# A hybrid layer (short convolution and HGRN2): attention and norm steps put into other slots, and one low half of the weights subtracted on chip instead of stored

## The chip, the cores and the metric

The kernel runs on one core of a Trainium2 chip. The metric is the device time of one execution in microseconds (us). The engines are TensorE (PE, with PEld for its weight loads), VectorE (DVE), ScalarE (ACT), GpSimd (POOL) and SyncE (SP). POOL and SP also issue DMA transfers.

## The reference

One encoder layer over a prompt of 2048 tokens and a separate sample of 64 tokens, width 1024. Cut to what matters here (8 heads of 128, chunks of 64 tokens):

```python
h = rms_norm(x, g_pre)
vA, bA, cA, zA, q, f, iv, zB, gA, gB = split_cols(h @ w_in)
u = cA * vA
yA = (silu(zA) * bA * causal_conv3(u, conv_w)) @ w_a_out
fg = lb + (1 - lb) * sigmoid(f); logf = log(fg); k = 1 - fg
q = silu(q) * K_B ** -0.5; v = iv
# hgrn2, for each chunk of 64 tokens, b = cumsum(logf) within the chunk:
att = causal((q * exp(b - ref)) @ (k * exp(ref - b)).T)
o = att @ v + (q * exp(b)) @ S
S = exp(b_last) * S + (k * exp(b_last - b)).T @ v
o = o * rsqrt(mean(o * o) + EPS) * g_onorm
yB = (o * silu(zB)) @ w_b_out
x = x + rms_norm((sigmoid(gA) * yA + sigmoid(gB) * yB) @ w_o, g_post)
x = x + (p @ w_ple_proj) * sigmoid(rms_norm(x, g_ple) @ w_ple_gate)
# returned: x of both, the last two columns of u and the last state S of both
```

## The kernel before

All activations stand feature-major (features on partitions, tokens along the row). The 2112 tokens run in three blocks of 768, 704 and 640 (block 0, block 1, the last block), each through the whole layer. Every product is split: an operand is cast to fp32r (`hi`) on ACT and the rest (`lo = x - hi`) is subtracted on DVE (`split`, L230). A weight block then takes three matmuls for each slice of k: hi by hi (L454), hi by the activations' lo (L455) and lo by hi (L456).

The projections work on pairs of column groups with seven products instead of eight (Strassen and Winograd's scheme): A11, S3, S1, S2, A12, A22, S4, where A11, A12 belong to the first column group, A21, A22 to the second, and S1 to S4 are sums of them. One product is 4 slices of k by 3 matmuls, 12 matmuls. `sgroup` runs such a group, `combined` gets its weights. In block 0 (`first`) the four raw halves are loaded, the sums are made on DVE, and the sums and the low halves are stored to DRAM through SP (`low<-lo` and `S<-s` in the views). Later blocks load what was stored (`kept_w`, `split_w`: raw half, cast on ACT, low half by a DMA); `used_later` tells which low halves are stored, and `spread` makes one be subtracted again. Raw, hi, lo and sum tiles come from rings of few buffers (5, 4, 4 and 3).

Path B runs head by head (`path_b`). `head_prep` does the groups of one head, FF/IV (forget gate and values) and ZB/QQ (output gate and queries), and starts the turning of keys and values: DVE transposes 32x32 pieces (L1067), POOL stores them (`tk<-r`, `tv<-r`, L1069), reads them back by token (`r<-tk`, L1074) and copies the keys side by side (L1080). The attention of the head runs while the next head's groups run: scores, then PE makes the state updates from keys and values (L1144), DVE scales and adds the states chunk by chunk (`p_state`, L1156 and L1159), and PE makes the outputs from scores and states (L1182, L1184). The outputs are normed, transposed back (`turn_o`, `to<-r`), read (`read_o`, `r<-to`) and multiplied with the output gate (`scale_o`, L1221).

These steps are placed by slots: after each product PE's group calls `hook`, which runs one slot's steps. A head has 21 slots in block 0 (a third group, of the gates, runs there) and 14 in the later blocks; `at(slot, step)` fills them. In block 0 there are also `piece`s in the slots: steps of `prepare_sums`, which make weight sums for later. The slots fix the order of PE's matmuls; around them a scheduler puts each engine's instructions in order. Each engine runs its instructions in that order, so a wait holds up all that stands behind it.

Between two blocks the norm of the finished block (L709, L721 are its transposes on PE) runs in the slots of the next block's first gate groups; `spread_out` takes the number of its steps for each slot from a row of figures.

Of the kernel before, what the change touches and what calls it, by code (L numbers as in the profile page):

```python
# [20 lines left out]
KB = D // P  # L21
# [10 lines left out]
VA, BA, CA, ZA, QQ, FF, IV, ZB, GA, GB = range(10)  # L32
# [62 lines left out]
def hybrid_step(  # L95
# [142 lines left out]
    def load_raw(src):  # L238
        raw = wp.tile([P, 4, P], F32, tag="raw", name=nm("raw"), bufs=5)
        SP.dma_start(raw, src)  # L240
        return raw
# [13 lines left out]
    def used_later(idx, part):  # L255

        if GA * 8 <= idx < GB * 8 + KB - 2:
            return part in ("S1", "S2", "S3", "S4")  # L260
        if idx in (GB * 8 + KB - 1, IV * 8):
            return part != 0
        if idx < QQ * 8:
            return part != 1
        if W_B <= idx < W_O:
            return part == 1 and idx - W_B >= KH
        return True

    def split_w(raw, key=None, spread=False, among_sums=False):


        hi = wp.tile([P, 4, P], F32R, tag="hi", name=nm("hi"))
        if spread:
            lo = low_tile()
            split(raw, hi, lo)
            return hi, lo
        if key in lows:
            lo = wp.tile([P, 4, P], F32R, tag="lo", name=nm("lo")) if among_sums else low_tile()
            A.copy(hi, raw)  # L279
            SP.dma_start(lo.bitcast(F32), lows[key])  # L280
            return hi, lo
        lo = wp.tile([P, 4, P], F32R, tag="lo", name=nm("lo"))
        split(raw, hi, lo)
        if key is not None and used_later(*key):
            lows[key] = dram.tile([P, 4, P], F32, tag=f"lo{key}", name=nm("low"), bufs=1)
            stores[0].dma_start(lows[key], lo.bitcast(F32))
        return hi, lo
# [53 lines left out]

    def kept_w(i1, i2, name, anew=False, spread=False):

        keys = dict(A11=(i1, 0), A12=(i1, 1), A22=(i2, 1))
        if name in keys:
            return split_w(load_raw(w_blk[keys[name]]), None if anew else keys[name], spread or keys[name][0] < QQ * 8 and keys[name][1] == 1)
        return split_w(load_raw(sums[i1][name]), (i1, name))

    def combined(i1, i2, first, anew):
# [598 lines left out]
    def head_prep(bl, hc, hd, first, hs, before):  # L948
# [22 lines left out]
        if hs and hd == 0:  # L971
            plain_group(FF * 8, IV * 8, hs, sink_f)
        else:
            sgroup(FF * 8 + hd, IV * 8 + hd, hc, sink_f, first)
        lg, staged_k, eq, staged_v = rt(), rt(turn * P), rt(), rt(turn * P)
        b, qx = staged_k[:, :n], staged_v[:, :n]
        wrote = [turned("tv", vt, staged_v, turn)]
# [248 lines left out]
    def path_b(bl, hc, first, kept, fills, hs, lead_sums=None):  # L1226


        def keep_z(hd, z):
            kept["o", hd] = spill("o", hd)  # L1230
            G.dma_start(kept["o", hd], z)

        slots, base, d = {}, 0, None
        if not first and not bl["last"]:
            next(fills)
        for hd in range(NH):
            d = head_prep(bl, hc, hd, first, hs, d)
            if first and hd > 0:
                next(fills, None)
            assert not hooks  # L1240
            attn = [head_attn(i, gs, d, hd) for i, gs in enumerate(bl["parts"])]
            scores = head_scores(bl["parts"], d)
            keep = partial(keep_z, hd, d["z"])
            piece = lead_sums and partial(next, lead_sums, None)

            def at(slot, *steps):
                slots.setdefault(base + slot, []).extend(s if callable(s) else partial(next, s) for s in steps if s is not None)

            if first:
                late = int(hd == 0)  # L1250
                at(2 + 2 * late, scores)
                for g in attn:
                    for slot in (6, 9, 12):
                        at(slot + late + (g is attn[1]), g)
                at(4 + late, partial(copy_k, d))
                at(15 + late, partial(turn_o, d))
                at(19 + late, partial(read_o, d))
                at(26 + late, partial(scale_o, d), keep)
                for slot in (8, 14, 20) if hd else (17,):
                    at(slot, piece)  # L1260
                if hd == NH - 1:
                    for slot in range(22, 94, 6):
                        at(slot, piece)
            else:
                for slot, steps in enumerate(((), (scores,), (), (), attn, (), attn)):
                    at(slot + 2, *steps)
                at(11, partial(turn_o, d))
                at(14, partial(read_o, d))
                at(14 + 7, partial(scale_o, d), keep)
                if hd == NH - 1:  # L1270
                    for slot in range(24, 108, 4):
                        at(slot, piece)
            count = 14 + 7 * first if hd + 1 < NH else 1 + max(slots) - base
            for slot in range(base, base + count):
                steps = slots.pop(slot, None)
                hooks.append(partial(each, steps) if steps else None)
            base += count
# [250 lines left out]
    def spread_out(*plans):  # L1528


        def steps(todo):
            with behind_all(m for m in copies + adds if m is not None):
                for gen, n in todo:
                    run(gen, n)

        for counts in zip_longest(*(plan for _, plan in plans), fillvalue=0):
            todo = [(gen, n) for (gen, _), n in zip(plans, counts) if n]
            hooks.append(partial(steps, todo) if todo else None)
# [131 lines left out]
    for bi, bl in enumerate(blocks):  # L1670
# [78 lines left out]
        if nxt:  # L1749
            xo.extend(stages[-1]["mid"])  # L1750
            fills = sized(nxt, gates(nxt, hc, kepts[bi + 1], False))
            norm = sized(bl, final_norm(bl, segs, xo, acc, h2, kept))
            spread_out((norm, (1, 1, 1, 1, 1, 1, 1, 0, 0, 0, 0, 1) + (0, 1) * KB + (0, 0, 1, 0, 0, 1) + (0, 1) * (KB - 1) + (1,)))
            run(fills, LEAD)
            assert not hooks
            run(final_gate(bl, segs, xo, h2, kept))
        else:

            gate = [final_gate(bl, [s], xo, h2, kept, anew=s is segs[1], held={} if s is segs[1] else {0: 0, 1: 0, 2: 0, 3: 2, 4: 0, 5: 4}) for s in segs]
            spread_out((norms[0], (2, 2, 1, 0, 1, 1, 4, 4)), (norms[1], (0,) * 6 + (1, 1) + (1, 1, 1, 0, 0, 1, 0, 1, 4, 4)))  # L1760
            run(ple(bl, ph, kept, spare=range(KB)))
            run(gate[0], 2)
            with behind_all(copies[:1]):
                run(norms[1], KB)
            run(gate[0])
            assert not hooks
            run(gate[1])
# [49 lines left out]
```

## Time and profile before

| what | value |
|---|---|
| time, median of three runs (lowest, highest) | 2527.51 us (2526.64, 2535.70) |
| the profiled execution's own time | 2528.36 us |
| its span in the profile | 2526.7 us |
| time around the span | 1.66 us |
| granted TensorE clock, mean | 0.999 |
| busy: PE, DVE, ACT, POOL | 2505.7, 1854.5, 1490.5, 477.6 us |
| DMA traffic | 761.36 MB, mean 301 GB/s |

The profile is of one execution. Block 0's heads run from about 99 to 475 us of the span, block 1's from about 1086 to 1345, the last block's from about 1860 to 2100. In a group's row stand line, engine, operation, output and input tiles, the size, the count, then busy us and mean ns, then the engine's idle us just before the group and what ended it.

### The profile page before, as it was taken

How to read it: one execution, taken by the hardware profiler on the slowest of the kernel's cores; microseconds unless marked ns; L12 is line 12 of the kernel's file. 1: busy time of each engine (PE TensorE's matmuls, PEld its weight loads, DVE VectorE, ACT ScalarE, POOL GpSimd, SP SyncE). 2: the span in 40 equal slices, each digit the busy share in tenths (PEclk: the TensorE clock that was granted, in tenths of full speed). 3: DMA queues.
4: the chain of work that ended last, by engine and by line, in shares of the span. 5: the costliest groups of instructions: out<-in, count | busy, mean ns of one | idle time of the engine just before them, and what ended most of it. 6: DMA issues, size and time to landing. Idle time of an engine off the chain costs nothing.

```text
span 2526.7 us, 47339 instructions
## 1 busy us (share of the span) xinstructions
PE 2505.7 (99%) x16302; PEld 2483.5 (98%) x16302; DVE 1854.5 (73%) x3575; ACT 1490.5 (59%) x2902; POOL 477.6 (19%) x819
## 2 busy tenths in 40 slices
PE   9999999999999999999999999999999999999999
PEld 9999999999999999999999999999999999999998
DVE  7898898998868775477775657978357775446967
ACT  6676676554453764466655556576356665546675
POOL 2032223221022021122223211102212221001011
PEclk9999999999999999999999999999999999999999
DMA  8789999997797798889989988989999998889986
GB/s 334 257 314 327 340 322 317 344 339 269 228 351 243 244 338 296 269 304 317 321 295 321 341 292 308 328 266 350 313 300 321 319 317 265 267 254 322 331 270 201
DMA packets 357873, 761.36 MB, mean 301 GB/s; under 512 B 44470, under 2 KB 49904, under 8 KB 357632
## 3 DMA queue, kind: packets, MB, share of 16 engines
q1 hardware_dynamic: 305856, 553.85, 64.8%
q0 software_dynamic: 51776, 204.48, 22.7%
q8 instruction: 128, 2.10, 0.3%
q14 instruction: 113, 0.93, 0.1%
HBM read 548.68 MB, written 209.47 MB: 300 GB/s over the span
## 4 chain that ended last, share of the span: by engine, by line
PE 87%; DVE 5%; DMA 4%; issue 2%; ACT 1%; POOL 1%; SPq 0%; DVEq 0%; ACTq 0%; POOLq 0%
PE pg L454 18%; PE pg L456 18%; PE pg L455 18%; PE pg L606 5%; PE pg L605 5%; PE pg L607 5%; PE pg L645 3%; PE pg L644 3%; PE pg L643 3%; DMA r<-tk 1%; PE pa L1144 1%; PE pa L1184 1%; PE pa L1182 1%; DMA low<-lo 1%; PE pa L1112 1%
## 5 line engine op out<-in xcount | busy, mean ns | idle before, releaser
L454 PE MATMUL pg<-r,hi 128*128 128x320 f32 (+2 forms) x3304 | 1076.5, 326 | 0.2 <-DVE r L502 0.2
L455 PE MATMUL pg<-r,hi 128*128 128x320 f32 (+2 forms) x3304 | 1067.4, 323 | 0.0
L456 PE MATMUL pg<-r,lo 128*128 128x384 f32 (+2 forms) x2380 | 777.1, 327 | 2.3 <-DMA lo<-low 1.2
L279 ACT CAST hi<-raw 128x512 fp32r<-128x512 f32 x658 | 405.0, 619 | 449.6 <-PE pg L455 186.3
L454 PEld LDWEIGHTS pg<-r,hi 128*128 128x128 f32 x3304 | 621.2, 188 | 2.5 <-issue 0.5
L455 PEld LDWEIGHTS pg<-r,hi 128*128 128x128 f32 x3304 | 621.7, 188 | 0.0
L456 PEld LDWEIGHTS pg<-r,lo 128*128 128x128 f32 x2380 | 447.2, 188 | 5.8 <-DVE lo L230 3.9
L230 ACT CAST hi<-raw 128x512 fp32r<-128x512 f32 x316 | 195.9, 623 | 179.6 <-PE pg L455 48.0
L456 PE MATMUL pg<-r,s 128*128 128x352 f32 (+1 forms) x924 | 291.7, 316 | 0.0
L606 PE MATMUL pg<-r,hi 128*128 128x320 f32 (+2 forms) x864 | 277.4, 322 | 0.3 <-DVE r L230 0.3
L605 PE MATMUL pg<-r,hi 128*128 128x320 f32 (+2 forms) x864 | 275.0, 322 | 0.0
L230 DVE TENSOR_TENSOR r<-r,r 128x320 fp32r<-128x320 f32 (+7 forms) x350 | 206.2, 608 | 42.9 <-ACT r L230 41.8
L230 DVE TENSOR_TENSOR lo<-raw,hi 128x512 fp32r<-128x512 f32 x263 | 180.2, 688 | 73.0 <-ACT hi L230 69.2
L230 ACT CAST r<-r 128x320 fp32r<-128x320 f32 (+7 forms) x350 | 183.8, 556 | 39.5 <-DVE r L1353 9.0
L607 PE MATMUL pg<-r,lo 128*128 128x352 f32 (+2 forms) x564 | 180.9, 321 | 0.4 <-DMA lo<-low 0.4
L456 PEld LDWEIGHTS pg<-r,s 128*128 128x128 f32 x924 | 173.5, 188 | 0.2 <-DVE s L230 0.2
L230 ACT CAST hi<-s 128x512 fp32r<-128x512 f32 x164 | 102.3, 624 | 120.7 <-PE pg L455 92.0
L644 PE MATMUL pg<-r,hi 128*128 128x384 f32 (+2 forms) x512 | 166.9, 327 | 0.2 <-DVE r L230 0.2
L643 PE MATMUL pg<-r,hi 128*128 128x384 f32 (+2 forms) x512 | 166.0, 328 | 0.2 <-ACT hi L279 0.2
L606 PEld LDWEIGHTS pg<-r,hi 128*128 128x128 f32 x864 | 162.1, 188 | 2.0 <-DVE r L230 1.5
L605 PEld LDWEIGHTS pg<-r,hi 128*128 128x128 f32 x864 | 161.3, 188 | 1.3 <-ACT r L230 0.8
L230 DVE TENSOR_TENSOR lo<-s,hi 128x512 fp32r<-128x512 f32 x164 | 112.4, 686 | 65.9 <-ACT hi L230 41.5
(383 smaller groups left out, 4174.5 us busy)
## 6 DMA issues: line engine op xcount, KB each, us to landing
raw<-w_blk SPq DMA_DIRECT2D x579, 256.0 KB, 4.6
raw<-S SPq DMA_DIRECT2D x436, 256.0 KB, 4.4
lo<-low SPq DMA_DIRECT2D x388, 256.0 KB, 4.4
s<-low SPq DMA_DIRECT2D x270, 256.0 KB, 4.8
low<-lo SPq DMA_DIRECT2D x239, 256.0 KB, 4.3
S<-s SPq DMA_DIRECT2D x152, 256.0 KB, 4.0
low<-r POOLq DMA_DIRECT2D x50, 256.0 KB, 5.0
r<-w_blk POOLq DMA_DIRECT2D x48, 256.0 KB, 7.1
```

What stands on the lines that cost most here:

```text
L230: return A.copy(hi, src).ins, V.tensor_tensor(lo, src, hi.bitcast(F32), ALU.subtract).ins
L279: A.copy(hi, raw)
L454: add(hi[:, k, :], xhi, start=start and k == 0, stop=False)
L455: add(hi[:, k, :], xlo, start=False, stop=False)
L456: last[0] = add(lo[:, k, :], xhi, start=False, stop=k == KH - 1).ins
L605: add(hi[:, k, :], xhi, start=start and k == 0, stop=False)
L606: add(hi[:, k, :], xlo, start=False, stop=False)
L607: last[0] = add(lo[:, k, :], xhi, start=False, stop=k == KH - 1).ins
L643: T.matmul(ps, hi[:, k % 4, :], xhi[:, c], start=k == ks[0], stop=False)
L644: T.matmul(ps, hi[:, k % 4, :], xlo[:, c], start=False, stop=False)
L645: last[0] = T.matmul(ps, lo[:, k % 4, :], xhi[:, c], start=False, stop=k == ks[-1]).ins
L1112: T.matmul(*unit, start=True, stop=True)
```

## The change

Four things. The low half of A22 of the groups FF/IV and ZB/QQ isn't stored in block 0 (`used_later`), and later blocks subtract it from the raw half on DVE (`among`); before, this was so only for the groups of lower number, path A's. The attention's steps from the states on come two slots later in block 0 and in the last block. In block 0 the pieces of `prepare_sums` move from slots 8, 14, 20 to 4, 10, 16. And one of the norm's early steps comes a slot later, with those behind it.

```diff
     def used_later(idx, part):
+        if idx // 8 in (QQ, IV) and part == 1:
+            return False
...
     def kept_w(i1, i2, name, anew=False, spread=False):
+        def among(idx, part):
+            return part == 1 and (idx < QQ * 8 or idx // 8 in (QQ, IV))
...
-            return split_w(load_raw(w_blk[keys[name]]), None if anew else keys[name], spread or keys[name][0] < QQ * 8 and keys[name][1] == 1)
+            return split_w(load_raw(w_blk[keys[name]]), None if anew else keys[name], spread or among(*keys[name]))
...
     # head_prep
-            sgroup(FF * 8 + hd, IV * 8 + hd, hc, sink_f, first)
+            sgroup(FF * 8 + hd, IV * 8 + hd, hc, sink_f, first, anew=hd == 0 and not bl["last"])
...
     # path_b, block 0 (first)
-                    for slot in (6, 9, 12):
+                    for slot in (6, 11, 14):
                         at(slot + late + (g is attn[1]), g)
                 at(4 + late, partial(copy_k, d))
-                at(15 + late, partial(turn_o, d))
-                at(19 + late, partial(read_o, d))
-                at(26 + late, partial(scale_o, d), keep)
-                for slot in (8, 14, 20) if hd else (17,):
+                at(17 + late, partial(turn_o, d))
+                at(21 + late, partial(read_o, d))
+                at(28 + late, partial(scale_o, d), keep)
+                for slot in (4, 10, 16) if hd else (17,):
                     at(slot, piece)
...
     # path_b, later blocks
-                for slot, steps in enumerate(((), (scores,), (), (), attn, (), attn)):
-                    at(slot + 2, *steps)
-                at(11, partial(turn_o, d))
-                at(14, partial(read_o, d))
-                at(14 + 7, partial(scale_o, d), keep)
+                late = 2 * bl["last"]
+                at(3, scores)
+                at(6 + late, *attn)
+                at(8 + late, *attn)
+                at(11 + late, partial(turn_o, d))
+                at(14 + late, partial(read_o, d))
+                at(21 + late, partial(scale_o, d), keep)
...
     # between blocks
-            spread_out((norm, (1, 1, 1, 1, 1, 1, 1, 0, 0, 0, 0, 1) + (0, 1) * KB + (0, 0, 1, 0, 0, 1) + (0, 1) * (KB - 1) + (1,)))
+            spread_out((norm, (1, 1, 1, 1, 1, 1, 0, 1, 0, 0, 0, 0, 1, 1) + (0, 1) * (KB - 1) + (0, 0, 1, 0, 0, 1) + (0, 1) * (KB - 1) + (1,)))
```

In instructions: SP issues 2078 where it issued 2126 (16 stores `low<-lo` and 32 loads of low halves fewer, 256 KB each), DVE runs 32 subtracts more, and the counts of PE, ACT and POOL are equal. On PE the matmuls L1182 and L1184 of every head of block 0 stand 24 matmuls later; in the last block so do L1144, L1182 and L1184; the norm's transposes L709 stand 12 rows later at both turns between blocks. Lines of the changed kernel have numbers five higher there than before.

The first place is DVE in the fourth head of block 0, where the states of the head before are scaled and added (L1159 before, L1164 now; `s_` and `lo_` are sums and low halves of weights). Before:

```order
L360 TENSOR_TENSOR s_3617<-raw_3605,raw_3607 128x512
L1221 TENSOR_TENSOR r_2040<-r_2852,r_2040 128x768
L230 TENSOR_TENSOR lo_3402<-s_3397,hi_3401 128x512
L495 TENSOR_TENSOR hf_3335<-hf_3217,pg_3234 128x384
L360 TENSOR_TENSOR s_3627<-raw_3607,raw_3609 128x512
L1156 COPY r_3343<-pa_3338 128x128
L1067 STREAM_TRANSPOSE r_3351<-r_3137 128x6x4x32
L1159 SCALAR_TENSOR_TENSOR r_3343<-r_3343,qc_2697,pa_3338 128x128 x3
L981 SCALAR_TENSOR_TENSOR r_3349<-keep,r_3348 128x768
L1159 SCALAR_TENSOR_TENSOR r_3447<-r_3343,qc_2697,pa_3444 128x128
```

And now:

```order
L230 TENSOR_TENSOR lo_3389<-s_3384,hi_3388 128x512
L500 TENSOR_TENSOR hf_3322<-hf_3198,pg_3216 128x384
L365 TENSOR_TENSOR s_3609<-raw_3589,raw_3591 128x512
L1161 COPY r_3330<-pa_3325 128x128
L1072 STREAM_TRANSPOSE r_3338<-r_3120 128x6x4x32
L1164 SCALAR_TENSOR_TENSOR r_3330<-r_3330,qc_2688,pa_3325 128x128
L1226 TENSOR_TENSOR r_2040<-r_2872,r_2040 128x768
L1164 SCALAR_TENSOR_TENSOR r_3330<-r_3330,qc_2688,pa_3325 128x128
L986 SCALAR_TENSOR_TENSOR r_3336<-keep,r_3335 128x768
L1164 SCALAR_TENSOR_TENSOR r_3330<-r_3330,qc_2688,pa_3325 128x128
```

The scale step of the head before (L1221, now L1226) stood ahead of the copy out of PSUM and the scan (L981, now L986) behind the third state; both now stand between the states.

The second place is DVE in the third head of block 1, from the reduced sums on to the transpose of the keys (L1067, now L1072), which opens their way to the state update. Before:

```order
L1012 TENSOR_TENSOR r_13947<-r_13737,r_13934 128x3x64
L1016 COPY r_13947<-hf_13946 128x128
L1018 TENSOR_TENSOR qc_13945<-qc_13945 128x5
L1067 STREAM_TRANSPOSE r_13935<-r_13947 128x6x4x32
L502 TENSOR_TENSOR r_13948<-hf_14005,hf_14024 128x352
```

And now, a row in the middle of the head and those at the transpose:

```order
L986 SCALAR_TENSOR_TENSOR r_13903<-keep,r_13902 128x704
L230 TENSOR_TENSOR s_13951<-raw_13948,hi_13950 128x512
L1173 TENSOR_SCALAR state_13899<-one_13892,r_13487 128x128
...
L1021 COPY r_13915<-hf_13914 128x128
L1023 TENSOR_TENSOR qc_13913<-qc_13913 128x5
L507 TENSOR_TENSOR r_13916<-hf_13973,hf_13992 128x352
L1072 STREAM_TRANSPOSE r_13903<-r_13915 128x6x4x32
```

The subtract of A22's low half (L230, into an `s` tile) is new between the scan and the states, and one step of the queries (L502, now L507) has come ahead of the keys' transpose.

The third place is POOL in a head of the last block (`to`, `tk`, `tv` are the turned outputs, keys and values in DRAM). Before:

```order
L1069 DMA to_24572<-r_24005 128x640
L1069 DMA tk_24540<-r_24399 128x640
L1074 DMA r_24498<-to_24572 128x4x160
L1074 DMA r_24610<-tv_24403 128x4x160
L1074 DMA r_24613<-tk_24540 128x4x160
L1080 COPY r_24615<-r_24613 128x640
```

And now:

```order
L1074 DMA tk_24480<-r_24350 128x640
L706 TENSOR_TENSOR ms_24510<-ms_24510,mhalf 128x4
L706 TENSOR_TENSOR ms_24519<-ms_24519,mhalf 128x1
L1079 DMA r_24578<-tv_24354 128x4x160
L1079 DMA r_24581<-tk_24480 128x4x160
L1074 DMA to_24571<-r_23956 128x640
L1085 COPY r_24583<-r_24581 128x640
L1079 DMA r_24509<-to_24571 128x4x160
```

The keys are now sent before the outputs, and the outputs are read back only behind the copy of the keys.

## The prediction

> **What bounds the kernel now.** I read the page first: the busy line, then the chain that ended last.
>
> ```profile
> span 2526.7 us, 47339 instructions
> PE 2505.7 (99%) x16302; PEld 2483.5 (98%) x16302; DVE 1854.5 (73%) x3575; ACT 1490.5 (59%) x2902; POOL 477.6 (19%) x819
> PE 87%; DVE 5%; DMA 4%; issue 2%; ACT 1%; POOL 1%; SPq 0%; DVEq 0%; ACTq 0%; POOLq 0%
> ```
>
> TensorE is busy 2505.7 of 2526.7 us, so it is the bound, and all its stops together are 21.0 us. The change alters no matmul (the instruction counts of PE are equal in the order of both kernels). So it can win back at most those 21 us and the little that PE loses around a stop; it can lose without such a limit. Next I read the groups of PE for what ends its stops. In a row the first pair of numbers is busy us and mean ns, the last part the idle us ahead of the group and its releaser.
>
> ```profile
> L456 PE MATMUL pg<-r,lo 128*128 128x384 f32 (+2 forms) x2380 | 777.1, 327 | 2.3 <-DMA lo<-low 1.2 <-DVE lo L230 1.0
> L1184 PE MATMUL pa<-r,r 128*128 128x128 f32 x208 | 41.2, 280 | 2.5 <-DVE r L1159 2.5
> L1144 PE MATMUL pa<-r,r 128*128 128x128 f32 x272 | 36.0, 276 | 4.3 <-POOL r L1080 4.2
> ```
>
> Three groups that the change can reach hold 9.1 of the 21 us: the attention's output waits for the states on DVE (L1184), the state update waits for POOL's copy of the keys (L1144), and projection products wait for the low half of a weight tile (L456). Windows tell where they lie.
>
> ```profile
> 99.00:475.00 376.00, 372.10 (x2410) 364.85 (x2409) 335.91 (x627) 248.74 (x521) 94.93 (x140) 1.00 0.90 322
> 452.00:700.00 248.00, 248.00 (x1459) 247.84 (x1456) 218.46 (x380) 130.10 (x266) 44.47 (x80) 1.00 0.84 289
> 1860.00:2100.00 240.00, 235.68 (x1825) 232.29 (x1824) 171.53 (x389) 154.97 (x271) 55.19 (x84) 1.00 0.94 317
> 2100.00:2300.00 200.00, 200.00 (x1361) 200.00 (x1360) 106.43 (x188) 104.35 (x198) 11.68 (x29) 1.00 0.82 262
> ```
>
> The columns are the window, then busy time of PE, PEld, DVE, ACT, POOL, then granted clock, DMA share, GB/s. The heads of block 0 (99 to 475) have 3.9 us of PE idle with DVE busy 89%; those of the last block (1860 to 2100) have 4.3. The other two rows, without a stop, give the pitch: 248.00/1459 = 0.170 us a matmul in block 0, 200.00/1361 = 0.147 in the last block. Two products are 24 matmuls, so a step put two products later gains 4.1 us in block 0 and 3.5 us in the last block.
>
> **Block 0: outputs two products later.**
>
> ```profile
> 118.33 0.49 PE L1184 MATMUL pa<-r,r 128*128 128x128 f32 x2 [1.61 <-DVE r L1159]
> 120.42 0.52 PE L456 MATMUL pg<-r,lo 128*128 128x384 f32 x1
> 120.74 0.52 PE L454 MATMUL pg<-r,hi 128*128 128x384 f32 x1
> 268.25 0.49 PE L1184 MATMUL pa<-r,r 128*128 128x128 f32 x2 [0.71 <-DVE r L1159]
> 418.96 0.49 PE L1184 MATMUL pa<-r,r 128*128 128x128 f32 x2 [0.19 <-DVE r L1159]
> 118.00:120.00 2.00, 1.67 (x7) 1.43 (x8) 2.00 (x8) 1.97 (x4) 0.00 (x0) 0.68 0.82 306
> 120.00:123.00 3.00, 3.00 (x13) 3.00 (x13) 1.88 (x7) 0.38 (x2) 0.00 (x0) 0.65 0.63 215
> ```
>
> These three stops, 1.61 + 0.71 + 0.19, are the 2.5 us of the group. All output matmuls of a head in block 0 stand 24 matmuls later in the new order, 4.1 us, while the state updates (L1144) stay. The steps on DVE are shuffled too. In the fourth head it looked like this:
>
> ```profile
> 266.23 0.28 DVE L1156 COPY r<-pa 128x128 f32<-128x128 f32 x1
> 267.89 1.06 DVE L1159 SCALAR_TENSOR_TENSOR r<-r,qc,pa 128x128 f32<-128x128 f32 x3
> 268.87 1.75 DVE L981 TENSOR_TENSOR_SCAN r<-keep,r 128x768 f32<-128x768 f32 x1
> 263.70 0.95 DVE L1221 TENSOR_TENSOR r<-r,r 128x768 f32<-128x768 f32 x1
> ```
>
> Now the scale step (0.95), which ran ahead of the copy L1156, and the scan (1.75) stand between the three states: the first two come no later, the third 1.75 us later, against a need 4.1 later, and the stop of 0.71 had to be made up first: 4.1 − 1.75 − 0.7 = 1.7 us to spare there. In the first head, whose stop is the longest, 4.1 − 1.6 leaves 2.5. So all three go: −2.5. Around a stop PE also loses 0.16 us of its rhythm (worked out below), three times: −0.5. And after the first stop alone the clock falls to 0.68 and 0.65: matmuls come 0.32 us apart (120.42, 120.74) instead of 0.17; over the seven or so that I count that slow, 7 × (0.32 − 0.17) = 1.1 us. Block 0: **−4.1**, bounds 0 (stops stay) and −4.1.
>
> The last block's first stop was as long, 1.65 us (quoted below), and cost no clock:
>
> ```profile
> 1913.00:1920.00 7.00, 6.61 (x51) 6.61 (x52) 5.34 (x10) 3.88 (x6) 2.05 (x4) 1.00 0.86 287
> ```
>
> So a stop of this length sometimes costs clock; where it did, I credit it. The Trainium skill ("TensorE: Matmul & The Clock Gate", "What's actually happening") has the gate fall to the half clock only after a whole idle window of about 3.4 us. By it a stop of 1.6 us would not touch the clock, the 1.1 us would have another cause and stay, and the sum would be 1.1 us smaller. The row with 1.00 agrees, those with 0.68 and 0.65 don't.
>
> **Last block: state update and outputs two products later.**
>
> ```profile
> 1911.44 0.31 PE L456 MATMUL pg<-r,lo 128*128 128x320 f32 x1
> 1913.39 0.38 PE L1144 MATMUL pa<-r,r 128*128 128x128 f32 x1 [1.65 <-POOL r L1080]
> 1929.33 0.54 POOL L1069 DMA_DIRECT2D tk<-r  x1 [3.02 <-DMA to<-r]
> 1929.86 0.77 POOL L1074 DMA_DIRECT2D r<-to  x1
> 1941.72 0.72 POOL L1080 COPY r<-r 128x640 f32<-128x640 f32 x1 [5.92 <-DMA r<-tk]
> ```
>
> The keys' chain takes 13.1 us from the issue of tk (1929.33) to the end of the copy (1942.44). In four of the eight heads PE waits for it, as at 1913.39; that is 4.2 of the 4.3 us of the L1144 group, and the other 0.1 lies in this window too. A start-to-start step of 1.95 (1911.44 to 1913.39) is a pitch of 0.15 plus 1.65 idle plus 0.16: the loss of rhythm. PE now comes 3.5 us later, and no stop was longer than 1.65, so 1.8 us or more are spare. Gain 4.3 + 4 × 0.16: **−4.9**, bounds 0 and −4.9. What the move endangers: on POOL the read-back r<-to now stands behind the copy, some 12.6 us later (1929.86 to 1942.44), and the scale step on DVE waits for it, with states behind it in DVE's order and PE behind those.
>
> ```profile
> r<-to POOLq DMA_DIRECT2D x16, 384.0 KB, 6.3
> 1946.43 0.82 DVE L1221 TENSOR_TENSOR r<-r,r 128x640 f32<-128x640 f32 x1
> ```
>
> It landed at about 1929.86 + 6.3 = 1936.2, so 10.3 us ahead of its use; the use moves 3.5 later: 10.3 − 12.6 + 3.5 = 1.2 us to spare, and the keys' transposes stand earlier on DVE than before, which adds some. I price it 0; gone, each us would cost about 1 us in seven heads.
>
> **The low half of A22 subtracted in all blocks.** Block 0 drops 16 stores and the others 32 loads of 256 KB: 12.6 of 761 MB. No PE stop of size waits for bandwidth, so this is 0 by itself; what it does to the stops for a low half:
>
> ```profile
> L456 PE MATMUL pg<-r,lo 128*128 128x384 f32 x617 | 209.7, 340 | 1.2 <-DVE lo L230 1.0
> L456 PE MATMUL pg<-r,lo 128*128 128x352 f32 x330 | 106.7, 323 | 1.2 <-DMA lo<-low 1.2
> ```
>
> The first is block 0 (99 to 475), where DVE waits less for buffers that a store holds: −0.5, half of it, bounds −1.2 and 0. The second (1040 to 1345) is a load of A12 that the change leaves: 0, bounds −1.4 (with its rhythm) and 0. In exchange 32 subtracts come onto DVE, 16 in each later block:
>
> ```profile
> L230 DVE TENSOR_TENSOR s<-raw,hi 128x512 fp32r<-128x512 f32 x53 | 36.4, 688 | 15.9 <-ACT hi L230 15.6
> L502 DVE TENSOR_TENSOR r<-hf,hf 128x352 f32<-128x352 f32 (+2 forms) x23 | 9.2, 400 | 0.5
> ```
>
> 16 × 0.69 = 11 us in 240 on an engine busy 71% there: no bound. They are split four products ahead of their use, so PE doesn't wait for them. But DVE runs in order, and in block 1 a subtract, and in six heads an L502 step (0.40) as well, now stand ahead of the transpose that opens the keys' chain: 0.69 in the first two heads, 1.09 in the rest. There PE is not moved, so the chain's slack must pay:
>
> ```profile
> 1091.60 0.82 POOL L1080 COPY r<-r 128x768 f32<-128x768 f32 x1 [5.92 <-PE pg L456]
> 1093.31 0.94 PE L1144 MATMUL pa<-r,r 128*128 128x128 f32 x7
> 1124.61 0.83 POOL L1080 COPY r<-r 128x768 f32<-128x768 f32 x1 [6.84 <-DMA r<-tk]
> 1125.63 1.50 PE L1144 MATMUL pa<-r,r 128*128 128x128 f32 x12
> 1316.43 0.83 POOL L1080 COPY r<-r 128x768 f32<-128x768 f32 x1 [7.01 <-ACT hi L279]
> 1319.56 1.50 PE L1144 MATMUL pa<-r,r 128*128 128x128 f32 x12
> ```
>
> From the copy's end to PE's start: 0.88 in the first head, 0.20 in the second, 2.30 in the last; all eight read so are 0.88, 0.20, 1.32, 0.88, 0.67, 1.24, 1.36, 2.30, together 8.9. Three heads fall short, by 0.49, 0.21 and 0.42, with three losses of rhythm: **+1.6**, bounds 0 (DVE often idles ahead of that transpose) and +8.6 (a delay of 2 us: seven heads, 7 × 2 − 6.5 + 7 × 0.16).
>
> **Norm steps.**
>
> ```profile
> L709 PE MATMUL pa<-ident,cols 128*128 128x128 f32 x6 | 0.9, 281 | 0.4 <-POOL cols L701 0.4
> ```
>
> This is the turn from block 1 to the last (1700 to 1720), where these transposes now stand 12 matmuls later: −0.5 with the rhythm, bounds −0.6 and 0. The one at the kernel's end isn't moved.
>
> **Sum.** −4.1 − 4.9 − 0.5 − 0.5 + 1.6 = −8.4 against the profiled execution's own 2528.36 (span 2526.7 and 1.66 around it): 2520.0. That execution lies 0.85 above the median of 2527.51, so on the median's scale **2519.1 us**. 0.5% is 12.6 us, about what a measurement of this kernel can tell from no change: faster is below 2514.9, slower above 2540.1. The forecast lies within.
>
> **Rivals.**
> A. Block 0's stops stay: DVE, busy 89%, gets pieces of the next sums earlier in a head (slots 4, 10, 16 for 8, 14, 20), and if one to three of them, at the 0.69 of a subtract of that size, come ahead of the states they eat the spare. For it: 1.7 us to spare in the fourth head. Against: the stores dropped. It decides from 1.7 to 2.5 us of lag and takes the 4.1 back: 2523.2. Chance 0.17.
> B. Slower: block 1's keys' chain becomes the stop. If transpose, POOL's issue and landing slip by 3 us in each head, PE waits 24 − 8.9 = 15.1 and loses 8 × 0.16 of rhythm: +16.4 instead of +1.6, so 2533.9. It decides from 2.3 us on, where the loss reaches the 10.0 gained elsewhere. For it: a copy that waits 6.84 us for its transfer with 0.20 us to spare. Against: the delay that the order shows is 1.1 us. Chance 0.12.
> C. Faster: no head of block 1 falls short (−1.6), and both stops for a low half go (−0.7 and −1.4): 2519.1 − 3.7 = 2515.4. Chance 0.13.
> That the change doesn't do what it says is excluded by the order but for its new flag for head 0, which moves no instruction.
>
> **Numbers.** Forecast 0.58, A 0.17, B 0.12, C 0.13. The range reaches from 2513.0 (C, with the 0.9 by which the fastest run lies under the median, and some more) to 2531.0 (past A, and the delay of 2 us with 2526.1; beyond it most of B). Faster: nearly half of C and some of the forecast's edge, 0.10. Slower by over 0.5% needs more than 4 us of delay in B: 0.07. Same 0.83.
>
> **What would show it.** Right: no idle before L1184 in 99 to 475, none before L1144 in 1860 to 2100, clock 1.00 in 118 to 123, about 1 us before L1144 in 1086 to 1345, PE idle some 13 us in all. Wrong: several us before L1144 in block 1 (B), L1184 still released by L1159 in block 0 (A), or in the last block DVE's L1221 released by r<-to.

## The result, and the profile after

The changed kernel takes 2521.27 us (median of 15 runs, 2519.55 to 2525.74); the kernel before, on the same chip, 2527.30 (15 runs, 2521.71 to 2535.70). The ratio is 0.9976 with a 95% interval of 0.9968 to 0.9984: 6.0 us less, between 4.0 and 8.1. The forecast was 2519.1, 8.4 less and within 0.5% of no change; the time lies in the range, 2.2 us above the forecast. Its terms came out less well than their sum.

From the page after:

```profile
span 2519.7 us, 47327 instructions
PE 2500.6 (99%) x16302; PEld 2481.2 (98%) x16302; DVE 1868.3 (74%) x3607; ACT 1489.6 (59%) x2902; POOL 480.7 (19%) x819
DMA packets 350961, 748.77 MB, mean 297 GB/s; under 512 B 43702, under 2 KB 49136, under 8 KB 350720
```

The profiled execution took 2521.40. The traffic is the 12.6 MB smaller and DVE does its 32 subtracts more, as the change says. PE's idle time is 19.1 us where it was 21.0, so stops have gone and others have come. The prediction gave some 13 us as a sign of being right, and that sign failed. The span fell by 7.0 us, so 5.1 of it lies in PE's busy time, with as many matmuls: taking a stop away can save more than its idle time (in the last block 5.3 us for 4.3 of idle, by the table below). The waits of PE, with us in total, times and the longest, first three of before and then those after:

```profile
PE pa L709 <- POOL cols L701: 1.9, 3, 0.8
PE pa L721 <- DVE r L744: 1.6, 3, 0.6
PE pg L456 <- DVE lo L230: 1.0, 4, 0.3
```

```profile
PE pg L461 <- DVE lo L230: 3.0, 2, 1.7
PE pa L726 <- DVE r L749: 2.8, 3, 1.4
PE pa L714 <- POOL cols L706: 1.7, 3, 0.8
...
PE pg L459 <- ACT hf L473: 1.2, 2, 0.7
...
PE pa L1149 <- POOL r L1085: 0.4, 1, 0.4
...
PE pa L1189 <- DVE r L1164: 0.2, 1, 0.2
```

The wait for the keys' copy fell from 4.2 to 0.4 (L1149 is the L1144 of before), the wait of the outputs for the states from 2.5 to 0.2 (L1189 for L1184). The wait for a low half that DVE makes (L461 for L456) is 3.0 in two stops where it was 1.0 in four short ones, and the wait of L726 (L721 before) grew from 1.6 to 2.8. The windows of two stretches of heads:

```profile
99.00:475.00 376.00, 370.87 (x2423) 365.85 (x2422) 336.24 (x629) 251.49 (x521) 98.92 (x143) 1.00 0.89 316
1860.00:2100.00 240.00, 240.00 (x1861) 237.92 (x1860) 179.59 (x412) 155.09 (x275) 57.80 (x86) 1.00 0.91 308
```

In the last block PE has no stop left (240.00 of 240.00, was 235.68). In block 0 it is idle 5.1 us, more than the 3.9 before. Here are the two new stops, of PE, and what DVE did ahead of the first (its work from 209.36 to 214.50 left out):

```profile
220.15 0.44 PE L461 MATMUL pg<-r,lo 128*128 128x384 f32 x1 [1.71 <-DVE lo L230]
271.17 0.44 PE L461 MATMUL pg<-r,lo 128*128 128x384 f32 x1 [1.30 <-DVE lo L230]
```

```profile
208.75 0.69 DVE L230 TENSOR_TENSOR lo<-s,hi 128x512 fp32r<-128x512 f32 x1 [4.38 <-DMA low<-lo]
...
214.50 0.28 DVE L1161 COPY r<-pa 128x128 f32<-128x128 f32 x1
214.70 1.53 DVE L1072 STREAM_TRANSPOSE r<-r 128x768 f32<-128x768 f32 x1
216.15 0.30 DVE L1164 SCALAR_TENSOR_TENSOR r<-r,qc,pa 128x128 f32<-128x128 f32 x1
216.37 0.95 DVE L1226 TENSOR_TENSOR r<-r,r 128x768 f32<-128x768 f32 x1
217.24 0.34 DVE L1164 SCALAR_TENSOR_TENSOR r<-r,qc,pa 128x128 f32<-128x128 f32 x1
217.50 1.75 DVE L986 TENSOR_TENSOR_SCAN r<-keep,r 128x768 f32<-128x768 f32 x1
219.17 0.32 DVE L1164 SCALAR_TENSOR_TENSOR r<-r,qc,pa 128x128 f32<-128x128 f32 x1
219.41 0.68 DVE L230 TENSOR_TENSOR lo<-raw,hi 128x512 fp32r<-128x512 f32 x1
```

From 208.75 on DVE is busy without a gap; the low half that PE wants (it ends at 220.09, PE starts at 220.15) stands behind the three states, the scale step and the scan. In the profile before, the low half for the same product came as late, behind the states and the scan too, and PE still took it without a stop:

```profile
219.58 0.68 DVE L230 TENSOR_TENSOR lo<-raw,hi 128x512 fp32r<-128x512 f32 x1
221.16 0.34 PE L456 MATMUL pg<-r,lo 128*128 128x384 f32 x1
```

What changed is the need. Before, this product stood behind two groups of outputs; now it stands ahead of them, 22 matmuls sooner (it begins with matmul 1320 of the program, not 1342). Moving the outputs two products back moves the products that were behind them forward, and those need their weights sooner. The prediction priced the first and not the second. That DVE stood 4.38 us for a store to free a buffer (3.71 in the same place before) may also make it late; what that wait is worth was not tried.

### The profile page after: what moved, and what is told of

Its sections match the earlier page's. It is cut to its first block, busy times and chain, and to the rows that moved or that the text cites. A ratio compares the mean times of both kernels' runs of the same rounds, so it can differ in the third digit from the quotient of the medians.

```text
span 2519.7 us, 47327 instructions
## 1 busy us (share of the span) xinstructions
PE 2500.6 (99%) x16302; PEld 2481.2 (98%) x16302; DVE 1868.3 (74%) x3607; ACT 1489.6 (59%) x2902; POOL 480.7 (19%) x819
## 4 chain that ended last, share of the span: by engine, by line
PE 88%; DVE 4%; DMA 3%; issue 3%; ACT 1%; POOL 0%; SPq 0%; DVEq 0%; ACTq 0%; POOLq 0%
PE pg L459 19%; PE pg L461 19%; PE pg L460 18%; PE pg L611 5%; PE pg L610 5%; PE pg L612 5%; PE pg L650 3%; PE pg L649 3%; PE pg L648 3%; DMA raw<-w_blk 1%; PE pa L1117 1%; PE pa L1187 1%; PE pa L1149 1%; PE pa L1189 1%; DVE lo L230 1%
## 5 line engine op out<-in xcount | busy, mean ns | idle before, releaser
L461 PE MATMUL pg<-r,lo 128*128 128x384 f32 (+2 forms) x2380 | 776.2, 326 | 3.3 <-DVE lo L230 3.0
L461 PEld LDWEIGHTS pg<-r,lo 128*128 128x128 f32 x2380 | 447.1, 188 | 5.4 <-DVE lo L230 4.2
L230 ACT CAST hi<-raw 128x512 fp32r<-128x512 f32 x348 | 215.6, 622 | 181.1 <-PE pg L460 48.2
L461 PE MATMUL pg<-r,s 128*128 128x352 f32 (+1 forms) x924 | 292.0, 316 | 0.0
L230 DVE TENSOR_TENSOR r<-r,r 128x320 fp32r<-128x320 f32 (+7 forms) x350 | 206.4, 608 | 45.0 <-ACT r L230 43.2
L230 DVE TENSOR_TENSOR lo<-raw,hi 128x512 fp32r<-128x512 f32 x264 | 181.1, 689 | 76.6 <-ACT hi L230 71.7
L230 ACT CAST r<-r 128x320 fp32r<-128x320 f32 (+7 forms) x350 | 183.8, 556 | 45.8 <-DVE r L403 11.9
L461 PEld LDWEIGHTS pg<-r,s 128*128 128x128 f32 x924 | 173.4, 188 | 0.0
L230 ACT CAST hi<-s 128x512 fp32r<-128x512 f32 x164 | 101.7, 623 | 115.4 <-PE pg L460 87.5
L473 ACT COPY hf<-pg 128x352 f32<-128x352 f32 (+2 forms) x354 | 157.0, 447 | 1.1 <-PE pg L461 1.1
```

Of the source, the lines that this page charges most:

```text
L230: return A.copy(hi, src).ins, V.tensor_tensor(lo, src, hi.bitcast(F32), ALU.subtract).ins
L461: last[0] = add(lo[:, k, :], xhi, start=False, stop=k == KH - 1).ins
L473: copied = A.copy(got[n], ps[bank])
```

## Reading many profiles side by side

One profile can't settle effects of 1 to 5 us, as the spread of the kernel before shows (14 us). But all kernels here have the same 16302 matmuls, and so the time from matmul number i to number j can be compared profile by profile. The stretches must begin and end where all kernels have done the same matmuls, so the first ends at 740, behind head 0's outputs in the old order and in the new: head 0's attention (500 to 740), the rest of block 0's heads (740 to 2990), the turn from block 0 to 1 (5250 to 5500), block 1's heads (6450 to 8500), the last block's heads (11750 to 13500). In us:

| profile | head 0 | rest of block 0 | turn | block 1 | last block |
|---|---|---|---|---|---|
| before | 38.93 | 351.32 | 40.40 | 284.67 | 229.31 |
| before, second time | 37.45 | 352.53 | 40.12 | 285.17 | 228.24 |
| only_norm | 37.42 | 350.00 | 40.14 | 285.17 | 226.27 |
| only_a22 | 38.03 | 350.83 | 40.11 | 284.89 | 224.70 |
| only_last | 37.47 | 353.63 | 40.21 | 284.67 | 223.59 |
| only_block0 | 35.05 | 355.49 | 41.39 | 285.16 | 226.12 |
| changed | 35.05 | 352.53 | 41.07 | 285.13 | 223.97 |
| scale26_keep | 35.05 | 354.89 | 40.44 | 286.21 | 223.30 |
| old_norm | 35.05 | 353.83 | 40.51 | 285.65 | 224.16 |
| b1_late | 35.05 | 351.27 | 41.27 | 284.62 | 223.45 |
| b1_one | 35.05 | 351.91 | 40.08 | 284.52 | 223.31 |
| b1_old_pieces | 35.05 | 357.76 | 43.48 | 284.61 | 223.44 |
| b1_old_block0 | 37.37 | 351.63 | 40.53 | 284.49 | 223.54 |
| b1_mix | 35.05 | 357.12 | 40.05 | 284.39 | 223.56 |

The names are those of the experiments below. Each kernel was timed against the kernel before on its chip; the ratios are to that, with their 95% intervals. Gains in us are differences of medians; the ratio is worked out otherwise and can lie an us or two away from them.

## The experiments

Four kernels had one part of the change alone.

**only_last**: the kernel before with the later slots of the last block.

```diff
+                late = 2 * bl["last"]
-                at(11, partial(turn_o, d))
+                at(11 + late, partial(turn_o, d))
...
```

> The kernel before with one part of the change: the attention's steps two products later in the last block. Theory 1 (the keys' copy on POOL was late there, and the later slots cover it): the idle time before the state update L1144 between 1860 and 2100 us, 4.2 us, goes, and with the rhythm PE lost around the four stops the kernel is 4.9 us shorter than before. Rival (the stops went because the change drops 16 loads in that block, so transfers land earlier): this kernel still has 3 us or more of idle there and is within 2 us of before.

2523.82 us, ratio 0.9981 (0.9972 to 0.9990). PE has no wait for the keys' copy left at all, and its last block takes 223.59 us. Theory 1's mechanism holds. In size, all nine profiles with the later slots have 223.3 to 224.2 there, mean 223.6; the five with the old slots 224.7 to 229.3, mean 226.9. By these means the part is worth 3.3 us; against the two profiles of the kernel before (mean 228.8) it is 5.2, and the whole time is 3.8 shorter. So the 4.9 of the forecast is not refuted: how long the old slots wait changes from one execution to the next.

**only_block0**: block 0's slots alone.

```diff
-                    for slot in (6, 9, 12):
+                    for slot in (6, 11, 14):
...
-                for slot in (8, 14, 20) if hd else (17,):
+                for slot in (4, 10, 16) if hd else (17,):
```

> The kernel before with one part of the change: block 0's slots (states, outputs, turn, read and scale two products later, pieces of the sums earlier). Theory 1: the three stops before L1184 (2.5 us, with clock and rhythm 4.1) go, but the projection products that now run ahead of the outputs need their low half sooner than DVE makes it, since DVE has the scale step and the scan between the states: about 3 us of stops before L456 come in their place, and the kernel is within 1.5 us of before. Rival (those new stops come from the low halves that are no longer stored): no L456 stop over 1 us here, and 4 us shorter than before.

2523.89 us, 0.9979 (0.9970 to 0.9987). The time is the rival's, 3.7 us less and not within 1.5; the stops are as Theory 1 has them:

```profile
PE pa L721 <- DVE r L744: 3.8, 3, 1.7
PE pg L456 <- DVE lo L230: 3.2, 3, 1.7
PE pa L1144 <- POOL r L1080: 2.4, 4, 1.1
```

The waits of the outputs are gone (0.2 is left) and the low half's are there, without the change's A22 part; so that part isn't their cause. The third row matters too: it is the keys' copy with the last block's slots untouched. Of its 2.4 us, 0.56 is a stop in block 0's last head and 1.8 lies in the last block, where the first profile had 4.2. The profile has less to show than the times: the rest of block 0 takes 355.49, among the longer ones, and the profiled execution (2526.34) is 2.5 us above this kernel's median.

**only_a22**: the low half of A22 subtracted in all blocks.

```diff
+        if idx // 8 in (QQ, IV) and part == 1:
+            return False
...
-spread or keys[name][0] < QQ * 8 and keys[name][1] == 1)
+spread or keys[name][1] == 1 and (keys[name][0] < QQ * 8 or keys[name][0] // 8 in (QQ, IV)))
```

> The kernel before with one part of the change: the low half of A22 of the heads' groups subtracted in all blocks and not stored. Theory 1 (traffic isn't the bound, and the subtracts stand ahead of the keys' transpose on DVE): 0 to 1.6 us longer, with a stop of 0.3 to 1.6 us before L1144 in block 1, and the last block's four stops of 4.2 us before L1144 as they were or longer. Rival (the 12.6 MB fewer relieve the transfers that PE waits for): 2 to 5 us shorter, with the keys' copy earlier in the last block.

2524.64 us, 0.9988 (0.9979 to 0.9997). Faster, not slower: 2.9 us, in the rival's 2 to 5. In its profile the wait for the keys' copy is 0.5 us in all, and the last block's heads take 224.70, the shortest with the old slots. That fits a relief of the transfers in the keys' chain, but it is one profile, and the next experiment got 226.27 without any such relief.

**only_norm**: the norm's plan alone.

```diff
-(1, 1, 1, 1, 1, 1, 1, 0, 0, 0, 0, 1) + (0, 1) * KB
+(1, 1, 1, 1, 1, 1, 0, 1, 0, 0, 0, 0, 1, 1) + (0, 1) * (KB - 1)
```

> The kernel before with one part of the change: the norm's steps in other slots. Theory 1 (the last sums of squares come a slot later on ACT and DVE while the transposes L721 that wait for them stay): the idle before L721 grows from 1.6 to about 2.8 us, the idle before L709 stays near 1.7, and the kernel is 1 to 2 us longer. Rival (my forecast: the transposes L709 find their means ready): idle before L709 falls by 0.4 and the kernel is 0.5 us shorter.

2524.92 us, 0.9990 (0.9981 to 0.9998). Theory 1 falls: the wait before L721 was 1.3 us and not 2.8. Of the rival's 0.4 us before L709 half came: at the turn from block 1 to the last the stop is 0.22 where it was 0.44. The same holds in all profiles, 0.43 to 0.45 in the six with the old plan and 0.20 to 0.22 in the eight with the new one, so this is an effect of the plan, of 0.2 us. The other turn did not move (40.14 us). What shortened this profile lies mostly in heads that the plan doesn't touch (the last block, 226.27). The parts alone, 3.8 + 3.7 + 2.9 + 2.7 us less, add up to 13.1, twice the whole; with intervals of about 2 us each way they can't be added. Whether part of each is the same stops of the last block isn't shown.

That called for the kernel before once more, and for three kernels near the changed one.

**before_again**: nothing edited.

> The kernel before once more, nothing edited, for a second profile of it. Theory 1 (the keys' chain of the last block ends within some tenths of a us of the moment PE needs it, so how long its four stops are changes from execution to execution, and the profile I argued from was one with long ones): times within 0.1% of before, idle before L1144 in the last block between 1.5 and 4.5 us and not 4.2 again, the stops of block 0 that wait for DVE's own order the same to 0.1 us. Rival (the stops are fixed by the program, and the parts tried alone each removed some): 4.2 us in four stops again.

2528.47 against 2528.23 us, ratio 1.0000 (0.9991 to 1.0009). Its second profile:

```profile
PE pa L1184 <- DVE r L1159: 3.5, 3, 1.6
PE pa L1144 <- POOL r L1080: 3.3, 5, 1.1
```

The keys' copy: 3.1 us in four stops in the last block (the other 0.2 is a stop in block 1) where it was 4.2 in four. Theory 1 holds for it. For block 0 it fell, by 1.0 us and by 0.8 more behind the copy L1156: the states' wait is not fixed either. Only the longest of the stops, 1.6 us in head 0, stands in every profile with the old slots.

**scale26_keep**: the changed kernel, scale step back in its old slot in block 0.

```diff
-                at(28 + late, partial(scale_o, d), keep)
+                at(26 + late, partial(scale_o, d), keep)
```

> The changed kernel with one slot undone: block 0's scale step at 26 and not 28, so that it runs ahead of the next head's state update and not among its states. Theory 1 (the scale step and the scan between the states push the low half of the next group's weights back on DVE, and PE waits for that at about 220 and 271 us): those two stops, 1.7 and 1.3 us, shrink by the 0.95 of a scale step each or go, and the kernel is 1.5 to 3.5 us shorter than the changed one, 7 to 9 shorter than before. Rival (the stops come from the pieces of the sums at slots 4, 10, 16): they stay.

2520.97 us, 0.9970 (0.9959 to 0.9981), not told apart from the changed kernel. One of the two stops is gone (the fourth head's), the third head's is 1.4 us, and new ones came:

```profile
PE pg L459 <- DVE hf L500: 2.7, 1, 2.7
PE pa L1189 <- DVE r L1164: 2.4, 2, 1.4
```

The rest of block 0 is 354.89, no better. In the third head the scale step's place matters little (1.4 for 1.7, where Theory 1 had 0.95 less); in the fourth it may be the cause.

**old_norm**: the changed kernel with the old norm plan (the diff of only_norm, undone).

> The changed kernel with the norm's steps where they were before. Theory 1 (the moved norm steps make the transposes of the sums wait for DVE at both turns between blocks): idle before them falls from 2.8 to about 1.5 us, the time at the two turns (850 to 950 and 1684 to 1730 us) falls by 0.7 and 1.2, and the kernel is 1 to 2 us shorter than the changed one. Rival (those stops change from execution to execution like the others): no fall, within 0.5 us.

2522.81 us, 0.9981 (0.9972 to 0.9989). No gain is shown, and none is excluded by the intervals. The idle before the L721 transposes is 1.9 where it was 2.8, so part of Theory 1's fall came; one profile can't tell it from the rival. In the table the turn takes 40.1 to 40.5 in all six profiles with block 0's old slots (mean 40.25) and 40.1 to 43.5 in the eight with the new ones (mean 41.04), whatever the norm plan. Why block 0's slots should reach so far was not tried.

**b1_late**: the changed kernel with the later slots in block 1 too.

```diff
-                late = 2 * bl["last"]
+                late = 2
```

> The changed kernel with the attention's steps two products later in block 1 too, not only in the last block. Theory 1 (in block 1 the keys' chain now ends 0.05 to 2.6 us ahead of need, and one head waits 0.4): no idle before L1149 in block 1, 0.7 us shorter than the changed kernel. Rival (as in block 0, products that now run ahead of the outputs wait for a low half that DVE makes later, or the read-back of the outputs behind the keys' copy comes too late for the scale step): 1 us or more of new stops in 1086 to 1345 us.

2519.75 us, 0.9966 (0.9955 to 0.9978), the lowest ratio of all. No idle before L1149 is left in block 1. The five kernels with this take 284.4 to 284.6 there; with A22 subtracted and the old slots (four profiles) 284.9 to 286.2, mean 285.5; without the subtract (five) mean 285.0. The later slots give 0.9 back. The means agree with 0.5 us for the subtracts, but only_a22, which has them alone, takes 284.89 without a stop, so that price isn't shown.

The last four go after the new stops of block 0, all from b1_late.

**b1_one**: outputs, turn, read and scale one product later in heads 1 to 7, two in head 0.

```diff
-                    for slot in (6, 11, 14):
+                    for slot in (6, 11 - bool(hd), 14 - bool(hd)):
...
-                at(28 + late, partial(scale_o, d), keep)
+                at(28 + late - bool(hd), partial(scale_o, d), keep)
```

> The kernel with the late slots in block 1 too, and in block 0 the outputs, turn, read and scale one product later than before in heads 1 to 7, not two; head 0 two as in the change. DVE's order then has the low half of A12 ahead of the states, and the scale step ahead of the copy out of PSUM. Theory 1 (PE's two stops of 1.9 and 1.5 us in the third and fourth head wait for exactly that low half, which the two-product move puts behind states, scale step and scan): both stops go, no more than one stop of 0.5 us or less before the outputs comes in their place, and 168 to 480 us is 1.5 to 3.5 us shorter than in the late-slots kernel's 311.3. Rival (the stops come from transfers of the weights): they stay.

2520.51 us, 0.9970 (0.9958 to 0.9983). DVE in the third head:

```profile
213.11 0.28 DVE L1161 COPY r<-pa 128x128 f32<-128x128 f32 x1
213.31 1.56 DVE L1072 STREAM_TRANSPOSE r<-r 128x768 f32<-128x768 f32 x1
214.77 0.68 DVE L230 TENSOR_TENSOR lo<-raw,hi 128x512 fp32r<-128x512 f32 x1
215.34 1.13 DVE L1164 SCALAR_TENSOR_TENSOR r<-r,qc,pa 128x128 f32<-128x128 f32 x3
```

```profile
PE pa L1189 <- DVE r L1164: 3.7, 3, 1.6
```

The low half stands ahead of the states now, and both stops are gone: the first half of Theory 1 holds. But 3.7 us of the outputs' wait for the states came in the second and seventh head, so the rest of block 0 is no shorter (351.91 against 351.27), and the second half fell.

**b1_old_pieces**: the pieces of the sums at their old slots.

```diff
-                for slot in (4, 10, 16) if hd else (17,):
+                for slot in (8, 14, 20) if hd else (17,):
```

> The kernel with the late slots in block 1 too, and in block 0 the pieces of the sums at 8, 14, 20 as before. The order still has the low half of A12 behind the states and the scan on DVE. Theory 1 (order of that low half against states and scan decides): the two stops of 1.9 and 1.5 us stay, within 0.5 us. Rival (the pieces' earlier slots load DVE and cause them): both go.

2522.30 us, 0.9973 (0.9964 to 0.9983).

```profile
PE pg L461 <- DVE lo L230: 6.9, 5, 2.6
```

The rival, that the early pieces cause the stops, falls: with the pieces late the low half of the third head stands behind the fourth state as well, and the wait is 6.9 us in place of 3.0. Theory 1's sizes fell too: the third head's stop is 2.6, the fourth's 0.2, and new ones of 1.5 and 2.4 came in the sixth and seventh. The rest of block 0 is 357.76, the longest of all. So by this profile the pieces' move in the change keeps the outputs' move bearable; the whole times (0.9973 against b1_late's 0.9966) don't tell the two apart.

**b1_old_block0**: the change without its block 0 part (the diff of only_block0, undone).

> The kernel with the late slots in block 1 too, and block 0's slots all as before: the change without its block 0 part. Theory 1 (that part gives 1.9 us in head 0, takes some 3.3 back in the stops for the low half of A12, and saves 2 to 2.5 us of stops before the outputs): within 1.5 us of the late-slots kernel (0.9966 of before), stops before L1184 or its like again 2.5 to 4.5 us, none for that low half over 0.5 us. Rival (my forecast, block 0's part is worth 4 us): 4 us longer than the late-slots kernel, 0.998 of before.

2522.70 us, 0.9979 (0.9969 to 0.9990). The outputs' wait is back at 3.2 us in four stops, the low half's wait at 1.0 in four, and the interval holds what both theories gave. By medians it is 2.9 us above b1_late, nearer to the 4 of the rival, which is my forecast, than to Theory 1's 1.5. In the table head 0 is 37.37 again.

**b1_mix**: one product later for the outputs of the third and fourth head, two for the others.

```diff
-                    for slot in (6, 11, 14):
+                    for slot in (6, 11 - (hd in (2, 3)), 14 - (hd in (2, 3))):
...
-                at(28 + late, partial(scale_o, d), keep)
+                at(28 + late - (hd in (1, 2, 3)), partial(scale_o, d), keep)
```

> The kernel with the late slots in block 1 too, and in block 0 the one-product move for the outputs of the third and fourth head alone (and the scale step of the second to fourth one product earlier than in the change), the two-product move for the others. DVE's order has the low half of A12 ahead of the states in those two heads, as in the kernel that moved seven heads by one product. Theory 1 (the stops of the two-product move lie in the third and fourth head, those of the one-product move in the second and seventh): none of either, 168 to 480 us at 308.5 to 310 where the two others had 311.3 and 312.0, and the kernel 2 to 3 us shorter than the late-slots one, 0.9955 to 0.996 of before. Rival (the scheduler's other shifts and transfers bring stops elsewhere in block 0): 311 us or more there, 0.9965 or more.

2520.68 us, 0.9975 (0.9965 to 0.9986). Both stops of the third and fourth head are gone and so are those of b1_one, and the rival is right all the same:

```profile
333.76 0.69 PE L459 MATMUL pg<-r,hi 128*128 128x384 f32 x1 [3.25 <-ACT r L1040]
331.00:334.00 3.00, 0.24 (x1) 0.24 (x2) 3.00 (x6) 2.97 (x6) 1.08 (x2) 0.79 0.95 358
334.00:337.00 3.00, 3.00 (x10) 3.00 (x11) 3.00 (x7) 3.00 (x14) 0.00 (x0) 0.50 0.95 300
337.00:340.00 3.00, 3.00 (x13) 3.00 (x12) 2.76 (x7) 2.96 (x10) 2.31 (x2) 0.57 0.71 250
```

One stop of 3.25 us at 334, behind ACT this time, with the clock at half from 332.74 on, within the stop, for 6.8 us. Of the kernels run, b1_late has the lowest time; its interval overlaps the changed kernel's, so that it beats it isn't shown.

## Why the prediction was right, and where it was not

**The bound.** Right as far as the loss could be placed: the stretches that changed are those whose stops of PE, or whose clock, changed. The sign of 13 us of idle failed (19.1), since new stops came for those that went.

**Last block, −4.9.** Right in kind; the size rests on one profile. The term took 4.2 us of idle from it; other profiles of the same slots have 3.1 (the second of before), 2.0 (only_norm), 1.8 (only_block0) and, with A22's loads dropped, 0.5 in this block. By the table the part is worth 3.3 to 5.2. What varies is the keys' chain that the prediction followed: for the second head it takes 15.4 us from the issue of tk to the end of the copy in the first profile, with a stop of 1.65 us behind it, and 13.6 in the second, with none. The read-back behind the copy did not come too late: the change's last block has no stop.

**Block 0, −4.1.** This is the step that failed. Head 0's stop went, in all eight profiles with the new slots: 35.05 us against a mean of 37.78, so −2.7. (The 1.1 us of clock belonged to the profiled execution alone, below; without that profile it is −2.5, more than the stop of 1.6 and the 0.16 of rhythm.) But "so all three go: −2.5" left out what moves the other way: the products that now run ahead of the outputs, and the low half that they need. The outputs' wait fell by 2.3 us in all and the low half's grew by 2.0. The rest of block 0 has a mean of 351.7 in the six profiles with the old slots and 353.3 in the four with the change's (changed, only_block0, old_norm, b1_late), +1.6, about as much as these vary. Together −1.1 in place of −4.1, and the turn to block 1 takes 0.8 back. The whole times say otherwise: 3.7 us less with this part alone, 2.9 more without it. So the stops that came are shown, and what the part is worth is not settled. Rival A named the right engine and place, and the wrong wait: pieces put back to their late slots made it worse.

**A22, +1.6.** Too large. One head of the changed kernel waits, 0.4 us, and the mean of the stretch with the subtracts is longer by 0.5, though not in only_a22. The three heads were counted from slack that one profile showed: the second head's 0.20 us was 1.26 in the second profile of the same kernel. Rival B stayed far off.

**Low halves, −0.5, and norm, −0.5.** The first is wrong: DVE's wait for a store got shorter in no way that PE shows, and the low half's wait went from 1.0 to 3.0 us for the reason above. The second is right in kind and half as large: 0.2 of the 0.4 us went at that turn. The steps that feed these transposes come a slot later too, which the term left out.

**The sum.** By the table the parts give −1.1 + 0.8 + 0.5 − 0.2 − 3.3 = −3.3, or −5.2 with the last block taken against the kernel before alone; measured are −6.0, with −4.0 to −8.1 as the interval. That −8.4 came so near is in part luck: terms from one profile, whose stops were other ones in the next. Where the other 1 to 3 us are saved is not settled; the traffic that the A22 part removes is a candidate, since that part alone measured 2.9 less, but the norm part alone, which has no such cause, measured 2.7.

## What to carry to other kernels

When a step is moved back in an engine's order, price what moves forward in its place: which operand it needs, and where that operand stands in the other engine's order. A chain that runs through transfers and ends about when it is needed gives a different stop in every execution: the last block's waits for the keys' copy came to 4.2, 3.1, 2.0 and 1.8 us, while the stop in head 0, behind DVE's own order, was 1.6 in all six profiles with the old slots. So take the worth of such a chain from several profiles. When two programs are compared by the number of a matmul, begin and end where both have done the same work. On a full engine, stops that are cleared head by head came back in other heads: the three arrangements of block 0 (b1_late, b1_one, b1_mix) can't be told apart by their times.

## What the hardware showed that I had not expected

The same stop of 1.6 us in head 0 costs clock in one execution and not in the next. In the first profile the clock after it was 0.68 and 0.65. In the second:

```profile
118.00:120.00 2.00, 1.85 (x12) 1.66 (x13) 2.00 (x6) 1.91 (x3) 0.00 (x0) 1.00 0.97 369
120.00:123.00 3.00, 3.00 (x22) 3.00 (x21) 2.58 (x9) 1.75 (x10) 0.00 (x0) 1.00 0.53 171
```

22 matmuls in the 3 us where the first had 13. Of the six profiles with block 0's old slots, which all have this stop, one lost clock. In only_block0 a stop of 1.7 us cost it again (0.56 over 219 to 222), in the changed kernel the same stop did not, and in b1_mix, with its stop of 3.25 us, it fell to 0.50. Over all 14 profiles, leaving out the first 100 us, the chance grows with the length: of 19 stops of 1.0 to 1.4 us none lost clock, of 18 of 1.4 to 1.8 us four did, and all five longer ones (2.1 to 3.25) did. Each time the clock then stood at half for 3.4 us (6.8 in b1_mix), here in the first profile:

```profile
118.71:122.12 3.41, 3.41 (x13) 3.17 (x13) 3.17 (x11) 1.61 (x3) 0.00 (x0) 0.50 0.91 325
```

The Trainium skill ("TensorE: Matmul & The Clock Gate", "What's actually happening") describes a window that runs freely, which agrees with a cost that changes with the moment, and asks for a whole idle window of about 3.4 us, which doesn't agree with the stops of 1.6 and 1.7 us. So a clock loss seen once behind a stop of 1.6 us is worth its chance, here four in 18, and not its size.
